# Where the layer norm of a convolution mixer is computed: beside the value projection or beside the key projection

## The chip, the cores and the metric

The kernel runs on one core of a Trainium2 chip. The metric is the device time of one execution in microseconds (us), the median of several runs. Engine names are those of the profile: PE is TensorE (its weight loads are listed apart as PEld), DVE is VectorE, ACT is ScalarE, POOL is GpSimd, SP is SyncE, which issues the DMAs.

## The reference, cut to what matters

One decoder layer for a sequence of 1024 tokens and a width of 1024, in float32. A joint input projection feeds four mixers of width 256 each; their outputs are concatenated, projected, added to the input, and a gated feed-forward block follows. The change concerns the third mixer (convolution, then layer norm and silu) and where it stands beside the fourth (attention):

```python
h = rms_norm(x, norm1_g)
z = h @ w_in
z_pool, s_b, s_c, s_h, c_a, c_g, zq, zk, zv = jnp.split(z, idx, axis=-1)
...
u = c_a * jax.nn.sigmoid(c_g)
u = causal_dwconv(u, conf_dw_w) + conf_dw_b
y_conf = jax.nn.silu(layer_norm(u, conf_ln_g, conf_ln_b))
...
y_attn = diff_attention(q, k, v, q_norm_g, k_norm_g, lam, lam_init, subln_g, rel_bias)
mix = jnp.concatenate([y_pool, y_sconv, y_conf, y_attn], axis=-1)
x = x + mix @ w_out
```

## The kernel before, in words

Every matmul is written as three (lines 138 to 140): each float32 operand is split into a high part and a low remainder, and high times high, high times low and low times high are added up in PSUM.

**Stages.** The tokens are eight blocks of 128, handled as four pairs p = 0 to 3. First come the norm and the channel-major projections of the three smaller mixers, with the long convolution (31 taps) on DVE; its result lies in `mixC`, channels on partitions. Then follow three token-major projections by `proj_tok` (line 468): keys (`use_k`), queries (`use_q`), values (`use_v`). For each pair `proj_tok` issues 48 matmuls of 128x256 and then calls its `use`. For keys and queries, `qk_norm` (line 482) copies the result out of PSUM, squares it (ACT), sums the squares (DVE, line 488), takes the power -1/2 on POOL (line 144, tile `r`) and scales (DVE, line 490); `stack_T` (line 493) splits the result and transposes it on PE (line 505). After the values, attention runs as 16 units `unit(u, p, h)` (line 652), one for each pair p and head h: scores on PE (line 668), bias and extremum on DVE (lines 675, 676), the exponential on ACT (line 679), the combination of the two maps on DVE (line 683), transposes on PE (line 694), their split on ACT and DVE (lines 698, 699), and the product with the values (line 703); after every second head the result is transposed back (line 715).

**What is moved.** `ln_pair(p)` takes the 256 tokens of pair p of `mixC` through layer norm and silu. It goes through five steps on four engines, each waiting for the one ahead:

```python
T.transpose(pt_[...], mixC[:, c, t * P:(t + 1) * P], ident)   # PE, L539, 4 of them
V.bn_stats(b6, pt_[...]); V.bn_aggr(mv[:, i, :], b6)          # DVE, L542, L543
rsqrt(rs, mv[:, :, 1], 1.0, 2)                                # POOL, L143, L144
V.tensor_scalar(ln[:, i, :], pt_[...], mv[...], rs[...])      # DVE, L548
T.transpose(pt_[...], ln[:, i, c * P:(c + 1) * P], ident)     # PE, L552, 4 of them
A.activation(th[:, c, :], src, AF.Tanh, ...)                  # ACT, L557
V.tensor_scalar(z, src, ...); V.scalar_tensor_tensor(z, ...)  # DVE, L558, L559
```

Its PSUM tile `lnp` has a single buffer, and its tile `th` shares the four buffers of tag `sp` with the keys' `kst` tiles and with the `sp` tiles named next.

**Filler work.** The part of the output projection that needs no attention is a generator, `gen_partial` (line 603). For each block of 128 tokens it splits the three finished mixer results `mixA`, `mixB` and `mixC` into `sp` tiles (ACT, DVE or POOL, lines 120, 122 and 622), issues 18 matmuls of 128x512 into PSUM tile `fm` (lines 599 to 601), and adds the input to the sum (lines 627, 628). `fill1` (line 636) hands these matmuls out between the instructions of the attention units, so many at each place as the table `FQ` says, and none of them may be issued ahead of the instruction at its place. Their weights are split in `wsplit` (tiles `whi` and `wlo`, line 134 on POOL).

**What sets the order.** All engines work through their instructions in order. The order is set at build time by a list scheduler: priority is the order in which the code issues, and an instruction that is not yet ready by the scheduler's own timing is passed over for a later one. So a filler matmul that has to wait for `mixC` slides to a later place on PE.

Of the kernel before, what the change touches and what calls it, by code (L numbers as in the profile page):

```python
# [66 lines left out]
def tile_hybrid(ctx, tc, x, norm1_g, w_in, pool_w, pool_scale, sconv_w, conf_w, conf_b, ln_g, ln_b,  # L67
# [74 lines left out]
    def rsqrt(dst, src, scale, n):  # L142
        G.tensor_scalar(dst, src, scale, EPS, op0=ALU.mult, op1=ALU.add)  # L143
        G.tensor_tensor(dst, dst, mhalf[:, 0:n], op=ALU.pow)  # L144
# [337 lines left out]
    def qk_norm(ps, z):  # L482
        A.copy(z, ps)
        sq = sm.tile([P, 512], F, name="sq", tag="sq")
        A.activation(sq, z, AF.Square)
        r = sm.tile([P, 16], F, name="r16", tag="r16", bufs=2)
        zv = z.rearrange("p (m d) -> p m d", d=32)
        V.tensor_reduce(r, sq.rearrange("p (m d) -> p m d", d=32), axis=AX.X, op=ALU.add)
        rsqrt(r, r, 1.0 / 32, 16)
        V.tensor_tensor(zv, zv, r.unsqueeze(2).broadcast_to([P, 16, 32]), op=ALU.mult)  # L490
        return zv

    def stack_T(kn, dst, isq, ps_new, nm, g, fill=None, p=None):
        for i in range(2):
            st = misc.tile([P, 4, 128], R, name="kst", tag="mi") if isq else spp.tile([P, 4, 128], R, name="kst", tag="sp")
            sv = st.rearrange("p m (a b d) -> p m a b d", a=2, b=2)
            src = kn[:, i, g * P:(g + 1) * P].rearrange("p (m d) -> p m d", d=32).unsqueeze(2).broadcast_to([P, 4, 2, 32])
            hi = sv[:, :, 0, :, :] if isq else sv[:, :, :, 0, :]
            lo = sv[:, :, 1, :, :] if isq else sv[:, :, :, 1, :]
            A.copy(hi, src)  # L500
            (G if isq and X3[2 * PO.index(p) + g] else V).tensor_tensor(lo, src, hi.bitcast(F), op=ALU.subtract)
            for m in range(0, 4, nm):
                ps = ps_new()
                for a in range(nm):
                    ins = T.transpose(ps[:, a * P:(a + 1) * P], st[:, m + a, :].bitcast(F), ident)
                if fill:
                    fill(ins)
                A.copy(dst[:, m:m + nm, i * P:(i + 1) * P], ps[:, 0:nm * P].rearrange("p (a b) -> p a b", a=nm))
# [5 lines left out]
        stack_T(qn[p], QT[p, g], True, ps_new, nm, g, fill, p)  # L514

    def use_k(p, ps):
        kn = qn[p]
        qk_norm(ps, kn.rearrange("p a b -> p (a b)"))
        for g in range(2):
            stack_T(kn, KT[g][:, :, p * 256:(p + 1) * 256], False, ps_t2, 4, g)  # L520
# [3 lines left out]
        V.tensor_tensor(qv, qv, gq.unsqueeze(1).broadcast_to([P, 16, 32]), op=ALU.mult)  # L524

    def use_v(p, ps):
        ln_pair(p)
        src = ps.rearrange("p (a d) -> p a d", d=64)
        vv = VV[p].rearrange("p i h d -> p (i h) d")
        A.copy(vv[:, :, 0:64], src)  # L530
        V.tensor_tensor(vv[:, :, 64:128], src, vv[:, :, 0:64].bitcast(F), op=ALU.subtract)

    def ln_pair(p):
        pt_ = psl.tile([P, 512], F, name="lnp", tag="lnp")
        mv = sm.tile([P, 2, 2], F, name="mv", tag="mv", bufs=2)
        for i in range(2):
            t = 2 * p + i
            for c in range(2):
                T.transpose(pt_[:, i * 256 + c * P:i * 256 + (c + 1) * P], mixC[:, c, t * P:(t + 1) * P], ident)  # L539
        for i in range(2):  # L540
            b6 = sm.tile([P, 6], F, name="b6", tag="b6", bufs=2)
            V.bn_stats(b6, pt_[:, i * 256:(i + 1) * 256])  # L542
            V.bn_aggr(mv[:, i, :], b6)  # L543
        rs = sm.tile([P, 2], F, name="rs", tag="rs", bufs=2)
        rsqrt(rs, mv[:, :, 1], 1.0, 2)
        ln = sm.tile([P, 2, 256], F, name="ln", tag="kn")
        for i in range(2):
            V.tensor_scalar(ln[:, i, :], pt_[:, i * 256:(i + 1) * 256], mv[:, i, 0:1], rs[:, i:i + 1],  # L548
                            op0=ALU.subtract, op1=ALU.mult)
        for c in range(2):  # L550
            for i in range(2):
                T.transpose(pt_[:, c * 256 + i * P:c * 256 + (i + 1) * P], ln[:, i, c * P:(c + 1) * P], ident)  # L552
        th = spp.tile([P, 2, 256], F, name="th", tag="sp")
        for c in range(2):
            z = mixC[:, c, p * 256:(p + 1) * 256]
            src = pt_[:, c * 256:(c + 1) * 256]
            A.activation(th[:, c, :], src, AF.Tanh, bias=lb[:, c:c + 1], scale=lg[:, c:c + 1])  # L557
            V.tensor_scalar(z, src, lg[:, c:c + 1], lb[:, c:c + 1], op0=ALU.mult, op1=ALU.add)  # L558
            V.scalar_tensor_tensor(z, th[:, c, :], 1.0, z, op0=ALU.add, op1=ALU.mult)  # L559

    proj_tok(C_K, use_k)
    proj_tok(C_Q, use_q, PO)
    for g in range(2):
        prep_q(PO[0], g, ps_t2, 4)
    proj_tok(C_V, use_v)

    hstk.close()
# [253 lines left out]
    for u in range(16):  # L821
        j, h = u // 4, u % 4
        p = PO[j]
# [355 lines left out]
```

## Time and profile before

| | us |
|---|---|
| median of 3 runs (lowest to highest) | 1107.63 (1106.45 to 1109.91) |
| the profiled execution | 1103.38 |
| its span, first to last instruction | 1101.6 |
| PE busy | 1059.2 |
| DVE busy | 739.1 |
| ACT busy | 440.5 |
| POOL busy | 223.2 |

The profiled execution is 4.25 us below the median of the runs. Busy times are sums over instructions; matmuls overlap one another in the pipeline, so PE busy is not PE at its peak. The stages that matter here are the token-major projections, which run from 172.5 to 251.7 us of the span, and the attention units behind them. The line that ends the sixth unit is the third group of line 715 matmuls.

### The profile page before, as it was taken

The page shows a single profiled execution, that of the slowest core. Times are in us where ns is not written, and L with a number is a line of the kernel's source. Part 1 is how long each engine was busy: PE and PEld are TensorE (multiplying, and loading weights), DVE is VectorE, ACT ScalarE, POOL GpSimd, SP SyncE. Part 2 cuts the span into 40 slices and gives each one's busy share as a digit, 9 for nine tenths or more (in the row PEclk, how much of TensorE's full clock was granted, in tenths as well). Part 3 has the DMA queues.
Part 4 walks back from the last instruction along what each step waited for, and adds up shares of the span by engine and source line. Part 5 has one row for each costly group of instructions (what it writes and reads, how often), then busy time and mean ns, then how long its engine had stood idle before and what let it go on. Part 6 is the DMA issues. An engine that isn't in the chain of part 4 may idle for free.

```text
span 1101.6 us, 13525 instructions
## 1 busy us (share of the span) xinstructions
PE 1059.2 (96%) x5203; PEld 882.0 (80%) x5203; DVE 739.1 (67%) x1127; ACT 440.5 (40%) x710; POOL 223.2 (20%) x202
## 2 busy tenths in 40 slices
PE   7989999997998989999999999999999999999998
PEld 7858889995777877777878888888888888888887
DVE  5599973458779996598667676565555656655540
ACT  5511213634567676542323333332333343433320
POOL 5224323653667653201000000000000000000000
PEclk9989999996999999999999999999999999999999
DMA  8131120110012121013567773233133168866731
GB/s 224 36 96 39 39 58 20 40 40 20 29 41 75 39 67 58 20 39 116 186 239 259 252 258 104 78 124 125 58 125 124 67 211 288 278 197 196 236 113 39
DMA packets 89664, 128.04 MB, mean 116 GB/s; under 512 B 17112, under 2 KB 57600, under 8 KB 87040
## 3 DMA queue, kind: packets, MB, share of 16 engines
q1 hardware_dynamic: 89600, 127.18, 35.4%
q8 instruction: 41, 0.67, 0.2%
q14 instruction: 23, 0.19, 0.1%
HBM read 94.13 MB, written 33.04 MB: 115 GB/s over the span
## 4 chain that ended last, share of the span: by engine, by line
PE 80%; DVE 9%; DMA 6%; ACT 2%; SPq 1%; POOL 1%; issue 1%; ACTq 0%; POOLq 0%; DVEq 0%
PE sb L140 10%; PE sb L138 10%; PE sb L139 10%; PE mm L140 6%; PE mm L139 6%; PE mm L138 6%; PE dx L138 3%; PE dx L139 3%; PE dx L140 3%; PE dy L139 2%; PE dy L138 2%; PE dy L140 2%; DMA dT<-wd 2%; PE fm L599 2%; DMA wd<-in_w_down_dram 2%; PE fm L601 2%
## 5 line engine op out<-in xcount | busy, mean ns | idle before, releaser
L138 PE MATMUL sb<-T,rhi 128*128 128x512 f32 x320 | 125.5, 392 | 0.0
L139 PE MATMUL sb<-T,rhi 128*128 128x512 f32 x320 | 125.4, 392 | 0.0
L140 PE MATMUL sb<-T,rlo 128*128 128x512 f32 x320 | 125.4, 392 | 0.0
L906 DVE TENSOR_TENSOR dq<-ds,dq 128x2048 fp32r<-128x2048 f32 x35 | 80.0, 2290 | 60.6 <-ACT dq L905 60.6
L905 ACT CAST dq<-ds 128x2048 fp32r<-128x2048 f32 x35 | 66.8, 1911 | 105.5 <-PE dy L140 39.5
L134 POOL TENSOR_TENSOR wlo<-st,whi 128x1024 fp32r<-128x1024 f32 (+2 forms) x30 | 73.9, 2466 | 103.9 <-ACT whi L120 97.6
L139 PE MATMUL mm<-hT,whi 128*128 128x512 f32 (+1 forms) x224 | 82.3, 372 | 0.7 <-DVE hT L200 0.7
L140 PE MATMUL mm<-hT,wlo 128*128 128x512 f32 (+1 forms) x224 | 81.9, 369 | 0.0
L138 PE MATMUL mm<-hT,whi 128*128 128x512 f32 (+1 forms) x224 | 80.0, 373 | 1.0 <-ACT hT L199 1.0
L312 DVE SCALAR_TENSOR_TENSOR t<-u,cw,t 128x1023 f32<-128x1023 f32 (+28 forms) x58 | 71.2, 1268 | 0.7
L139 PEld LDWEIGHTS sb<-T,rhi 128*128 128x128 f32 x320 | 60.1, 188 | 13.5
L138 PEld LDWEIGHTS sb<-T,rhi 128*128 128x128 f32 x320 | 60.1, 188 | 13.5 <-DVE tp L1025 0.3
L140 PEld LDWEIGHTS sb<-T,rlo 128*128 128x128 f32 x320 | 60.0, 188 | 13.5
L905 ACT CAST rhi<-st 128x1024 fp32r<-128x1024 f32 x28 | 29.4, 1051 | 85.6 <-PE sb L139 44.6
L140 PE MATMUL dx<-dq 128*128 128x512 f32 x160 | 62.3, 390 | 0.0
L139 PE MATMUL dx<-dq 128*128 128x512 f32 x160 | 62.2, 389 | 0.0
L138 PE MATMUL dx<-dq 128*128 128x512 f32 x160 | 61.8, 389 | 0.0
L138 PE MATMUL mm<-whi,hT 128*128 128x256 f32 x192 | 55.0, 288 | 0.0
L140 PE MATMUL mm<-whi,hT 128*128 128x256 f32 x192 | 54.9, 287 | 0.0
L679 ACT ACTIVATE pt<-sc,mx 128x128 f32<-128x128 f32 (+7 forms) x64 | 47.6, 745 | 17.6 <-DVE mx L676 17.1
L139 PE MATMUL mm<-wlo,hT 128*128 128x256 f32 x192 | 54.5, 284 | 0.0
L120 ACT CAST whi<-st 128x1024 fp32r<-128x1024 f32 x28 | 29.4, 1049 | 61.6 <-PE mm L139 50.2
(342 smaller groups left out, 2705.2 us busy)
## 6 DMA issues: line engine op xcount, KB each, us to landing
ds<-dL SPq DMA_DIRECT2D x35, 512.0 KB, 4.1
wd<-in_w_down_dram SPq DMA_DIRECT2D x10, 1024.0 KB, 5.0
dT<-wd SPq DMA_DIRECT2D x10, 1024.0 KB, 4.0
dL<-afs SPq DMA_DIRECT2D x10, 1024.0 KB, 3.9
ds<-dT SPq DMA_DIRECT2D x20, 512.0 KB, 5.7
st<-in_w_in_dram SPq DMA_DIRECT2D x18, 512.0 KB, 3.8
st<-in_w_gate_dram SPq DMA_DIRECT2D x15, 512.0 KB, 4.1
st<-in_w_up_dram SPq DMA_DIRECT2D x15, 512.0 KB, 3.6
```

Source lines behind the costliest of these rows:

```text
L120: A.copy(dst, src)
L134: G.tensor_tensor(lo[:, nv:], st[:, nv:], hi[:, nv:].bitcast(F), op=ALU.subtract)
L138: T.matmul(ps, lhsT=L[0], rhs=Rr[0], start=first, stop=False, skip_group_check=more)
L139: T.matmul(ps, lhsT=L[0], rhs=Rr[1], start=False, stop=False, skip_group_check=more)
L140: return T.matmul(ps, lhsT=L[1], rhs=Rr[0], start=False, stop=last, skip_group_check=more)
L312: V.scalar_tensor_tensor((z if s == 30 else acc)[:, s:], u[:, :S - s], w[:, 30 - s:31 - s], acc[:, s:], op0=ALU.mult, op1=ALU.add)
L599: yield lambda: T.matmul(ps, lhsT=L[0], rhs=Rr[0], start=first, stop=False)
L601: yield lambda: T.matmul(ps, lhsT=L[1], rhs=Rr[0], start=False, stop=last)
L679: A.activation(pts[m][:, 0:w], sc[:, 0:w], AF.Exp, bias=mx, scale=-1.0, accum_out=lt[:, h, m, i:i + 1])
L905: A.copy(hi, src)
L906: (eng or V).tensor_tensor(lo, src, hi.bitcast(F), op=ALU.subtract)
```

## The change

The call of `ln_pair(p)` moves from the head of `use_v` to the head of `use_k`: the layer norm of a pair is now issued with the keys of that pair and ahead of what the keys need, rather than with its values. No instruction is added, dropped or changed in size.

```diff
     def use_k(p, ps):
+        ln_pair(p)
         kn = qn[p]
         qk_norm(ps, kn.rearrange("p a b -> p (a b)"))
...
     def use_v(p, ps):
-        ln_pair(p)
         src = ps.rearrange("p (a d) -> p a d", d=64)
```

The scheduler turns this into another order on PE, DVE, ACT and POOL; the DMA queue of SP stays the same. First, PE where the value projection (`mm`) ends and attention (`sc`) begins, before: `lnp` is the layer norm's PSUM tile, and no filler matmul (`fm`) is near.

```order
L140 MATMUL mm<-whi,hT_104 128x256
L668 MATMUL sc<-KT_1364,QT 128x256 x2
L539 MATMUL lnp<-ident,mixC 128x128 x4
L668 MATMUL sc<-KT_1364,QT 128x256 x3
L694 MATMUL tp<-ident,pt 128x128
L668 MATMUL sc<-KT_1364,QT 128x256 x2
L694 MATMUL tp<-ident,pt 128x128 x2
L552 MATMUL lnp<-ident,ln 128x128 x4
L703 MATMUL av<-at,VV_1375 128x256
```

The same place on PE in the changed kernel:

```order
L140 MATMUL mm<-whi,hT_104 128x256
L668 MATMUL sc<-KT_1364,QT 128x256
L599 MATMUL fm<-whi,sp 128x512
L600 MATMUL fm<-wlo,sp 128x512
L601 MATMUL fm<-whi,sp 128x512
L599 MATMUL fm<-whi,sp 128x512
L600 MATMUL fm<-wlo,sp 128x512
L601 MATMUL fm<-whi,sp 128x512
L599 MATMUL fm<-whi,sp 128x512
L668 MATMUL sc<-KT_1364,QT 128x256 x2
```

The transposes of pairs 2 and 3 (16 matmuls into `lnp`) have left the attention stage, and filler matmuls stand between the first scores. Up to the first group of line 715 there were 0 filler matmuls and are now 36; up to the second 54 and now 58; up to the third 101 in both. From there on the two orders of PE are alike but for a few neighbours that change places.

Second, POOL in the projections, before: `r_...` are the keys' sums of squares, one tile for each pair, `rs` is the layer norm's own, `wlo` a low part of weights.

```order
L143 TENSOR_SCALAR rs<-mv 128x2
L144 TENSOR_TENSOR rs<-rs,mhalf 128x2
L143 TENSOR_SCALAR r_1447<-r_1447 128x16
L144 TENSOR_TENSOR r_1447<-r_1447,mhalf 128x16
L143 TENSOR_SCALAR r_1540<-r_1540 128x16
L144 TENSOR_TENSOR r_1540<-r_1540,mhalf 128x16
L143 TENSOR_SCALAR r_1633<-r_1633 128x16
L144 TENSOR_TENSOR r_1633<-r_1633,mhalf 128x16
L134 TENSOR_TENSOR wlo<-st,whi 128x1024 x2
```

And POOL there in the changed kernel:

```order
L143 TENSOR_SCALAR r_1598<-r_1598 128x16
L143 TENSOR_SCALAR rs<-mv 128x2
L144 TENSOR_TENSOR r_1598<-r_1598,mhalf 128x16
L144 TENSOR_TENSOR rs<-rs,mhalf 128x2
L143 TENSOR_SCALAR r_1720<-r_1720 128x16
L144 TENSOR_TENSOR r_1720<-r_1720,mhalf 128x16
L134 TENSOR_TENSOR wlo<-st,whi 128x1024 x2
L143 TENSOR_SCALAR rs<-mv 128x2
L143 TENSOR_SCALAR r_1842<-r_1842 128x16
L144 TENSOR_TENSOR rs<-rs,mhalf 128x2
L144 TENSOR_TENSOR r_1842<-r_1842,mhalf 128x16
```

The layer norm's small steps on POOL now stand behind the keys' powers and, for pair 2, behind two weight splits. On PE the projections now hold all 32 transposes of `lnp` instead of 16. Between the last line 539 matmul of a pair and its first line 552 matmul PE now has 66 projection matmuls and 16 transposes of line 505 for pair 1, 49 and 8 for pair 2, 42 and 8 for pair 3, and 48 projection matmuls for pair 0.

## Rows read from the trace of the kernel before

**Rows 1.** From the page: busy times; granted clock in 40 slices.
```profile
PE 1059.2 (96%) x5203; PEld 882.0 (80%) x5203; DVE 739.1 (67%) x1127; ACT 440.5 (40%) x710; POOL 223.2 (20%) x202
...
PEclk9989999996999999999999999999999999999999
```

**Rows 2.** Stretches: length, busy us and instructions of PE, PEld, DVE, ACT, POOL; clock.
```profile
172.50:251.70 79.20, 79.20 (x670) 78.93 (x669) 38.31 (x63) 35.62 (x70) 40.47 (x29) 1.00 0.11 34
...
251.70:311.40 59.70, 49.41 (x232) 40.28 (x231) 47.11 (x156) 33.15 (x96) 34.90 (x43) 0.83 0.10 29
```

**Rows 3.** PE in time at three places: start, duration, line, tiles, count.
```profile
251.71 0.41 PE L668 MATMUL sc<-KT,QT 128*128 128x256 f32 x2
...
278.63 0.63 PE L599 MATMUL fm<-whi,sp 128*128 128x512 f32 x1
...
311.25 0.60 PE L715 MATMUL tp<-ident,oT 128*128 128x128 f32 x4
```

**Rows 4.** Waits of PE from 251.7 to 311.4: total us, times, longest.
```profile
PE sc L668 <- ACT pt L679: 5.8, 4, 2.4
```

**Rows 5.** Stretches in which the clock was halved, columns as in rows 2.
```profile
256.65:273.70 17.05, 12.86 (x49) 10.10 (x50) 13.49 (x57) 9.10 (x31) 3.05 (x7) 0.50 0.05 17
277.10:280.50 3.40, 3.23 (x9) 2.65 (x10) 2.54 (x11) 1.53 (x5) 0.73 (x1) 0.50 0.00 0
```

**Rows 6.** The chain: one group of `lnp` transposes at full clock.
```profile
240.58 0.44 PE lnp L539 x4
```

**Rows 7.** DVE groups of the layer norm, 251.7 to 311.4: busy us, mean ns.
```profile
L558 DVE TENSOR_SCALAR mixC<-lnp,lg,lb 128x256 f32<-128x256 f32 x4 | 2.1, 538 | 0.0
L559 DVE SCALAR_TENSOR_TENSOR mixC<-th,mixC 128x256 f32<-128x256 f32 x4 | 2.0, 502 | 0.0
L548 DVE TENSOR_SCALAR ln<-lnp,mv,rs 128x256 f32<-128x256 f32 x4 | 2.0, 537 | 0.0
...
L542 DVE BATCH_NORM_STATS2 b<-lnp 128x6 f32<-128x256 f32 x4 | 1.5, 418 | 0.5 <-PE lnp L539 0.5
...
L543 DVE BATCH_NORM_AGGREGATE mv<-b 128x2 f32<-128x6 f32 x4 | 0.5, 160 | 0.0
```

**Rows 8.** Layer norm of pair 1 in time, from its first PE to its DVE step.
```profile
240.42 0.60 PE L539 MATMUL lnp<-ident,mixC 128*128 128x128 f32 x4
...
243.66 1.00 DVE L548 TENSOR_SCALAR ln<-lnp,mv,rs 128x256 f32<-128x256 f32 x2 [1.10 <-POOL rs L144]
```

**Rows 9.** POOL groups, 172.5 to 251.7: busy us, mean ns.
```profile
L144 POOL TENSOR_TENSOR r<-r,mhalf 128x16 f32<-128x16 f32 x8 | 23.3, 2914 | 0.7
L134 POOL TENSOR_TENSOR wlo<-st,whi 128x1024 fp32r<-128x1024 f32 x6 | 14.9, 2485 | 14.8 <-ACT whi L120 9.3 <-DVE whi L122 5.4
```

**Rows 10.** POOL and DVE in time where both split operands.
```profile
197.50 5.04 POOL L134 TENSOR_TENSOR wlo<-st,whi 128x1024 fp32r<-128x1024 f32 x2 [0.47 <-ACT whi L120]
...
198.84 3.99 DVE L501 TENSOR_TENSOR kst<-qn,kst 128x256 fp32r<-128x256 f32 x2 [1.09 <-ACT kst L500]
...
203.34 0.75 DVE L501 TENSOR_TENSOR kst<-qn,kst 128x256 fp32r<-128x256 f32 x2
```

**Rows 11.** Two stretches of attention behind the sixth unit, columns as in rows 2.
```profile
311.40:350.00 38.60, 32.71 (x190) 26.67 (x188) 33.75 (x90) 28.27 (x65) 25.82 (x22) 1.00 0.18 60
350.00:400.00 50.00, 50.00 (x288) 43.22 (x287) 46.52 (x103) 35.15 (x72) 29.91 (x34) 1.00 0.15 49
```

**Rows 12.** Two filler matmuls in time at full clock.
```profile
281.77 0.39 PE L599 MATMUL fm<-whi,sp 128*128 128x512 f32 x1
282.00 0.40 PE L600 MATMUL fm<-wlo,sp 128*128 128x512 f32 x1
```

**Rows 13.** Six units in three stretches that end at line 715; columns as rows 2.
```profile
251.70:269.50 17.80, 10.53 (x42) 7.64 (x40) 15.82 (x60) 8.42 (x29) 6.03 (x6) 0.64 0.10 30
269.50:294.10 24.60, 21.85 (x95) 18.00 (x96) 17.96 (x62) 13.51 (x40) 13.30 (x18) 0.85 0.07 22
294.10:311.40 17.30, 17.03 (x98) 14.65 (x97) 13.32 (x35) 11.21 (x28) 15.56 (x20) 1.00 0.13 36
```

## The prediction

> **What bounds the kernel now.** I read the page first. PE is busy 96% of the span, DVE 67%, and the row of granted clocks has its dips at the start and in the tenth slice, where the attention stage begins [rows 1]. So PE's order is what counts, and the place to look at is where PE has gaps or a low clock. Then I read the stretches. In the token-major projections, 172.5 to 251.7 us, PE is busy all of the 79.2 us, at 0.118 us for each of its 670 instructions, while DVE is busy 38.3 and POOL 40.5 us [rows 2]. In the first six attention units, 251.7 to 311.4 us, PE is busy 49.4 of 59.7 us, so 10.3 us are gaps, and the mean clock is 0.83 [rows 2]. The timeline shows why: the first scores run at 251.7 us, the first filler matmul at 278.6 us [rows 3]. In these 27 us PE has little but the units' own chain to do (score, extremum on DVE, exponential on ACT, back to PE), and its longest sum of waits is 5.8 us for the exponential [rows 4]. The filler matmuls need `mixC`, whose layer norm for pairs 2 and 3 is still being worked on between the units.
>
> The clock tells the same. PE runs with 1.00, the upper of its two levels (2.4 GHz), in the projections; in the first 5 us of attention it is mostly idle; then the clock is at 0.50 (1.2 GHz) from 256.65 to 273.70 us and again from 277.10 to 280.50 us [rows 5]. Behind 280.5 us, with filler matmuls on PE, it stays at 1.00. The two stretches at 0.50 hold 12.86 + 3.23 = 16.1 us of busy PE.
>
> **The change, part by part.** The profiled execution took 1103.38 us, 1.8 us of it outside its span; the sum is made against it, and I carry its difference over to the median of the runs, 1107.63 us, 4.25 us higher.
>
> *Work that goes to the projections.* The 16 transposes of pairs 2 and 3 now run there. PE is full there, so they lengthen the stage: four groups of four at 0.44 us [rows 6] are 1.8 us, plus 1.8 us on the end. DVE gets 2.1 + 2.0 + 2.0 + 1.5 + 0.5 = 8.1 us more [rows 7], and ACT four `th` steps; with 38.3 us of 79.2 used, DVE has room, so I cost this at nothing, as the projection matmuls cover it, unless PE has to wait for it, which is the next term.
>
> *A wait that may be added.* PE takes its instructions in order, so behind a line 552 transpose that waits for `ln` stand the projection matmuls of the next pairs, and all the later stages behind them. In the trace the way from the first line 539 matmul to the end of line 548 takes 240.42 to 244.66, 4.2 us [rows 8]. PE now has 82 instructions between them for pair 1, 57 for pair 2, 50 for pair 3 and 48 for pair 0: at 0.118 us, 9.7, 6.7, 5.9 and 5.7 us of cover. POOL's `rs` steps, however, now stand behind the keys' power of 2.9 us [rows 9]. If that is in the way each time, the chain is 7.1 us: 0.4 us short for pair 2 and 1.2 us for pair 3. Lower bound 0, upper bound of this case 1.6; neither row is nearer, so I take 0.8 us.
>
> On DVE there is a row that speaks against the move: two line 501 steps took 3.99 us while POOL split weights for 5.04 us, and 0.75 us right after [rows 10], 3.2 us more. The Trainium skill, "SBUF — State Buffer", section "Who interferes with whom", gives a reason: a DVE instruction with two SBUF inputs and a GpSimd instruction that reads SBUF use one shared port pair, and the one that starts first holds it throughout. By that rule line 559, with `th` and `mixC` as inputs, can be held up too, and there is more of POOL's long work beside it in the projections; the trace agrees for line 501. By the row, and by the rule, the sum stays as it is as long as the layer norm is not what PE waits for; if it is, this is the last rival below.
>
> *Work that leaves the first six units, and the fillers.* The fillers' inputs are ready when attention begins: 36 of the 101 filler matmuls stand in the first two units instead of none, and 101 in all six as before. What PE has to do there: 49.4 us, less half of the 16.1 us at half clock (8.0), less the 1.8 us of moved transposes, leaves 39.6 us. DVE: 47.1 less 8.1 leaves 39.0 us. How long do they take together? Lower bound: PE without a gap, 39.6 us. Two stretches right behind show units and fillers interleaved from a table at full clock [rows 11]: from 350 to 400 us PE has no gap and DVE is 93% busy, which would give 39.0 / 0.93 = 41.9 us; from 311.4 to 350 us PE is 85% busy and DVE 87%, which would give 39.6 / 0.847 = 46.7 us. Upper bound: the gaps stay, 59.7 less 1.8 = 57.9 us. The nearest row is the stretch that follows at once, with units as small as these: I take 46.7 us. That is 13.0 us less than 59.7.
>
> The weights for the fillers are split at the start of attention (DVE `whi`, then POOL `wlo`) as before; the first filler group has its weights from the queries' buffers and doesn't wait for them. The second and third groups wait for a POOL split of 2.5 us each [rows 9]; I cost that inside the 85%.
>
> *Sum.* 13.0 − 1.8 − 0.8 = 10.4 us less: 1093.0 for an execution like the profiled one, 1097.2 for the median. Behind the sixth unit PE's order is the same, so what is won there is not given back: the feed-forward part is bound by PE without gaps, whenever it starts.
>
> **The rivals.**
>
> *The fillers get in the way.* A filler that stands ahead of a score or a transpose on PE delays the unit's chain, and at 0.23 us apiece [rows 12] 36 of them are 8.3 us in a stretch that took 17.8 us [rows 13]. If none of it falls into gaps, the first two units take 26.1 us; the second stretch, with 22 instead of 54 fillers, is 7.4 us shorter and the third 0.9 us, and nothing is won by filling. What is left is the clock: 8.0 − 1.8 − 0.8 = 5.4 us, 1102.2 us. For it: the chain's steps are short and each needs PE four times. Against it: POOL, ACT and DVE all have gaps in 251.7 to 269.5 us, and PE 7.3 us of them [rows 13].
>
> *The clock falls all the same.* The first scores still wait for DVE behind the two `whi` casts, and later fillers for POOL; if PE has a gap like that of 251.7 to 256.65 us again, the 8.0 us are not won: 13.0 − 8.0 − 2.6 = 2.4 us, 1105.2 us. Against it: seven fillers stand between the first and the second score.
>
> *Better than the sum.* PE and DVE as from 350 to 400 us: 59.7 − 41.9 − 1.8 = 16.0 us less, 1091.6; without any gap 18.3, 1089.3.
>
> *Slower: the layer norm stalls the projections.* Place: the line 552 transposes of pairs 1 to 3. Price: if `rs` waits for a power (2.9) and for two weight splits (5.0), and DVE is held up once (3.2), the chain is 4.2 + 11.1 = 15.3 us, and PE waits 5.6 + 8.6 + 9.4 = 23.6 us. That leaves 13.0 − 1.8 − 23.6 = −12.4: 1120 us. It decides from the point where the three waits together exceed 11.2 us, that is, a chain of about 11 us for each pair on average. For it: POOL's order has `rs` of pair 2 behind two splits. Against it: that is one pair of four, and POOL is busy only half of the stage.
>
> **How the numbers follow.** Forecast and better 0.64, fillers in the way 0.17, clock falls 0.10, both of these 0.03 (the 2.6 us of cost alone, 1110.2), slower 0.06. A measurement of this kernel can tell 0.3%, 3.3 us, from no change: faster means below 1104.3, slower above 1111.0. The first two cases are faster, less a small part of the second: 0.78. The clock's case and both together are no change: with that part 0.15. Slower: 0.07. The forecast's own range is 1091 to 1102; to leave out no more than 2 in 10 the range reaches from 1090, near the gapless bound, to 1105.5, past the clock's case.
>
> **What would show it.** In the changed profile: line 552 matmuls of all pairs before the end of the values, which should come some 2 to 3 us later than 251.7; first filler right behind the first score; clock at 1.00 from the start of attention; third group of line 715 at about 301 us instead of 311.25; the rest shifted as a block. Wrong: waits of line 552 on `ln` of several us in the projections, a stretch at 0.50 behind 254 us, or waits of the scores and transposes that grow by as much as the fillers take.

## The result and the profile after

| | before | after |
|---|---|---|
| median (lowest to highest), us, 4 runs each | 1107.04 (1104.86 to 1109.91) | 1091.78 (1088.75 to 1097.45) |
| profiled execution, us | 1103.38 | 1092.04 |
| first line 539 matmul of the projections to first score | 80.91 | 82.56 |
| first score to third group of line 715 (six units) | 59.54 | 45.35 |
| third group of line 715 to the end of the span | 790.35 | 789.9 |

The changed kernel takes 0.9867 of the time of before, 95% interval 0.9820 to 0.9913: 15.3 us between the medians. The forecast was 1097.2 us, the range 1090 to 1105.5.

In the page after, PE and the granted clock answer to [rows 1]. DVE and PE are busy some 5 us less in all, and the dip of the clock in the tenth slice is gone.

```profile
span 1090.2 us, 13509 instructions
...
PE 1054.3 (97%) x5203; PEld 875.9 (80%) x5203; DVE 734.6 (67%) x1127; ACT 439.4 (40%) x710; POOL 224.1 (21%) x202
...
PEclk9989999999999999999999999999999999999999
```

The stretches of the changed kernel, with the columns of [rows 2] (length, then busy us and instructions of PE, PEld, DVE, ACT, POOL, then clock, DMA share, GB/s): the projections, the six units, the three parts of the units that end at line 715 (they answer to [rows 13]), and the one piece at half clock (it answers to [rows 5]).

```profile
172.40:255.00 82.60, 82.60 (x694) 81.62 (x693) 44.49 (x84) 38.75 (x77) 47.70 (x38) 1.00 0.11 33
255.00:300.30 45.30, 41.94 (x214) 33.07 (x213) 38.78 (x129) 28.84 (x87) 30.45 (x34) 0.96 0.13 41
...
255.00:272.70 17.70, 14.96 (x66) 11.10 (x65) 14.16 (x50) 8.82 (x33) 9.77 (x9) 0.90 0.15 46
272.70:283.30 10.60, 10.24 (x58) 8.08 (x57) 9.21 (x33) 8.35 (x26) 6.16 (x7) 1.00 0.07 25
283.30:300.30 17.00, 16.75 (x94) 13.89 (x93) 15.41 (x47) 11.67 (x30) 14.52 (x19) 1.00 0.15 47
...
262.60:266.00 3.40, 3.40 (x13) 2.81 (x14) 2.09 (x10) 2.04 (x7) 0.08 (x1) 0.51 0.03 7
```

PE is still busy through the whole of the projections. The first and the third part of the units are about as long as before (17.7 and 17.0 us, against 17.8 and 17.3); nearly all of the gain is in the second, 10.6 us for 24.6. The first part takes no longer although 36 filler matmuls now run in it, and the second has work left for 10.6 us only. The gaps of PE in the units are 45.3 − 41.9 = 3.4 us instead of 10.3, and the clock is halved for 3.4 us instead of 20.5.

PE in time in the changed kernel (start, duration, line, tiles), which answers to [rows 3]: the filler runs right behind the first score, and line 715 comes at 300.33.

```profile
254.98 0.28 PE L668 MATMUL sc<-KT,QT 128*128 128x256 f32 x1
255.09 0.40 PE L599 MATMUL fm<-whi,sp 128*128 128x512 f32 x1
...
300.33 0.60 PE L715 MATMUL tp<-ident,oT 128*128 128x128 f32 x4
```

The waits of PE from 255 to 300.3 us in the changed kernel (what it waited for: us in all, times, longest) answer to [rows 4]. The wait for the exponential has shrunk from 5.8 to 1.5 us, and no other has taken its place.

```profile
PE tp L694 <- DVE pt L683: 1.5, 3, 0.8
PE sc L668 <- ACT pt L679: 1.5, 2, 0.8
PE tp L505 <- POOL kst L501: 0.3, 1, 0.3
```

**What the first filler waited for in the kernel before.** The prediction said: for `mixC`. The first filler matmul, however, belongs to token block 0, which is in pair 0, and the layer norm of pair 0 had ended in the projections (the last of its line 559 steps at about 234 us). In the kernel before, DVE and POOL in time show what came right before 278.63 us:

```profile
272.87 0.43 DVE L122 CAST sp<-mixC 128x256 fp32r<-128x256 f32 x1
...
275.25 0.72 POOL L622 TENSOR_TENSOR sp<-mixB,sp 128x256 fp32r<-128x256 f32 x1
...
277.65 0.54 DVE L558 TENSOR_SCALAR mixC<-lnp,lg,lb 128x256 f32<-128x256 f32 x1
```

DVE reads `mixC` for the filler's token block at 272.87 us, ahead of pair 3's last steps, and all operands of that block were split by 275.97 us (the first filler's own, the high part of `mixA`, by 273.56). At 278.19 us line 558 of pair 3 ends, the last instruction that reads `lnp`, and 0.44 us later the filler runs. PE shows no idle time right before it: the scheduler had put it behind the score that runs at 278.03 us, so this trace alone doesn't show what held it. PSUM space is given out by pools, in the order in which they are opened. The projections' pools end and attention's begin in the same space (lines 96 and 97, 575 to 577):

```python
psm = psA.enter_context(pool("psm", 3, space=PSUM))   # mm, three buffers
psl = psA.enter_context(pool("psl", 1, space=PSUM))   # lnp
...
psp = psB.enter_context(pool("psp", 2, space=PSUM))   # tp
psq = psB.enter_context(pool("psq", 1, space=PSUM))   # av
psf = psB.enter_context(pool("psf", 1, space=PSUM))   # fm: the fourth buffer, as lnp was
```

So `fm` would take over the buffer of `lnp` and have to wait until the layer norm of all pairs is through with it. That became the theory to test.

### The profile page after: what moved, and what is told of

Same layout as the page of the kernel before. It is cut to its first block, busy times and chain, and to the rows that moved or that the text cites. A ratio compares the mean times of both kernels' runs of the same rounds, so it can differ in the third digit from the quotient of the medians.

```text
span 1090.2 us, 13509 instructions
## 1 busy us (share of the span) xinstructions
PE 1054.3 (97%) x5203; PEld 875.9 (80%) x5203; DVE 734.6 (67%) x1127; ACT 439.4 (40%) x710; POOL 224.1 (21%) x202
## 4 chain that ended last, share of the span: by engine, by line
PE 78%; DVE 11%; DMA 6%; ACT 2%; issue 1%; POOL 1%; SPq 0%; ACTq 0%; POOLq 0%; DVEq 0%
PE sb L140 10%; PE sb L138 10%; PE sb L139 10%; PE mm L139 6%; PE mm L140 6%; PE mm L138 6%; PE dx L140 3%; PE dx L139 3%; PE dx L138 3%; PE dy L140 3%; PE dy L139 2%; PE dy L138 2%; DMA wd<-in_w_down_dram 2%; DMA dT<-wd 2%; DVE pt L683 1%
```

## The experiments

Three theories. B: the fillers wait for the PSUM buffer of `lnp`. M, that of the prediction: they wait for the data in `mixC`. L: the fillers' place matters little; the gain is that the layer norm's 8.1 us of DVE work [rows 7] leave the units. The first four kernels ran on one chip beside the kernel before (1107.25 us, 26 runs); the last four on another (1105.4 us, 13 runs).

**1. Layer norm of pairs 2 and 3 still in attention, in another buffer** (kernel before; the `tp` tiles, of which there are two).

```diff
     def use_v(p, ps):
-        ln_pair(p)
+        p < 2 and ln_pair(p)
...
-    def ln_pair(p):
-        pt_ = psl.tile([P, 512], F, name="lnp", tag="lnp")
+    def ln_pair(p, ps_n=None):
+        pt_ = ps_n() if ps_n else psl.tile([P, 512], F, name="lnp", tag="lnp")
...
+    ln_pair(2, ps_tp), ln_pair(3, ps_tp)
```

> The kernel before (layer norm beside the values), but pairs 2 and 3 are issued at the head of attention and take a buffer of the transposes' PSUM tile tp instead of lnp, so that the last reader of lnp is pair 1's and not pair 3's. The layer norm of pairs 2 and 3 stays among the attention units. Theory B (bank): the filler matmuls waited for lnp, because their tile fm takes over its PSUM bank; here fillers start right behind the first scores, the clock stays up, and most of the gain comes: 1095 to 1101 us against 1107, a little less than the change gives since 8.1 us of DVE work stay in the units. Theory M (the prediction's: fillers wait for mixC of pairs 2 and 3): fillers start as late as before, about 1105 to 1108. Theory L (load: what counts is that the layer norm's steps leave the units): 1105 to 1108.

Measured: 1098.88 us (1096.18 to 1100.36), ratio 0.9919 [0.9893, 0.9946]. The first filler comes 14.1 us behind the first score instead of 26.9, the units take 53.2 us, and the clock is halved for 13.7 us. The wait has not gone but moved, onto the buffer that the layer norm now uses. In its trace, PE in time (in brackets the idle time before, and what ended it):

```profile
266.28 0.88 PE L694 MATMUL tp<-ident,pt 128*128 128x128 f32 x3 [1.13 <-DVE mixC L558]
266.81 0.78 PE L599 MATMUL fm<-whi,sp 128*128 128x512 f32 x1
```

A unit's transposes wait for line 558, and the filler stands behind them. The filler runs ahead of the end of the last line 558, at 268.50 us, which fits B. But with two buffers the layer norm also ends earlier, 15.8 us behind the first score instead of 26.5, so this kernel doesn't tell the buffer from an earlier layer norm. The time lies in B's range, though B's fillers right behind the first scores did not show.

**2. Fillers that read no `mixC`** (kernel before).

```diff
-            for kg, mix in enumerate((mixA, mixB, mixC)):
+            for kg, mix in enumerate((mixA, mixB, mixB)):
```

> The kernel before, but the fillers read mixB a second time in place of mixC (so the output lacks the convolution mixer's part). Everything else, the layer norm beside the values too, stays. Theory M (fillers wait for mixC): fillers start at once at the beginning of attention and the time falls to 1093 to 1098 us. Theory B (bank of lnp): the first filler still stands behind the last layer norm step, near 278 us, and the time is 1104 to 1108 us. Theory L (load of the layer norm in the units): 1104 to 1108 us.

Measured: 1108.8 us (1103.29 to 1113.93), ratio 1.001 [0.9986, 1.0033]. In its trace, in time, the last split of an operand, line 558 of pair 3, and the first filler:

```profile
275.47 0.72 POOL L622 TENSOR_TENSOR sp<-mixB,sp 128x256 fp32r<-128x256 f32 x1
...
277.87 0.53 DVE L558 TENSOR_SCALAR mixC<-lnp,lg,lb 128x256 f32<-128x256 f32 x1
...
278.85 0.63 PE L599 MATMUL fm<-whi,sp 128*128 128x512 f32 x1
```

The fillers no longer need anything of the layer norm's result and still come behind its last reading of `lnp`, 26.9 us behind the first score as before. M is refuted as the cause. The time is 0.8 us above the range of B and L, which expected the same here, so this kernel doesn't tell the two apart.

**3. The changed kernel, fillers held back** (the first 26 entries of `FQ` are zero, the 27th is 52; the layer norm stays early).

```diff
-FQ = [13, 0, 1, 0, 4, 0, 0, 0, 0, 0, 5, 6, 1, 4, 0, 0, 0, 0, 6, 1, 2, 5, 1, 0, 3, 0, 0, 2, ...
+FQ = [0, 0, 0, 0, 0, 0, 0, 0, 0, 0, 0, 0, 0, 0, 0, 0, 0, 0, 0, 0, 0, 0, 0, 0, 0, 0, 52, 2, ...
```

> The changed kernel (layer norm beside the keys), but the table that hands out the fillers gives none at its first 26 places and all of these at the 27th, so that by the order PE has 0 fillers in the first two units, 58 up to the second and 101 up to the third group of line 715, nearly as before (0, 54, 101). Theory B and M (the gain is fillers in the gaps, with the clock that this holds up): most of the gain goes, 1102 to 1108 us, and the clock is at half again for 10 us or more behind 256 us. Theory L (load): it stays, 1090 to 1096 us.

Measured: 1097.32 us (1094.29 to 1102.35), ratio 0.9921 [0.9895, 0.9948], between the two. Its stretches, columns as above, in the three parts that end at line 715:

```profile
255.06:270.30 15.24, 8.56 (x29) 5.74 (x27) 12.15 (x46) 7.02 (x27) 4.84 (x3) 0.67 0.11 35
270.30:289.70 19.40, 19.38 (x93) 16.47 (x94) 10.63 (x38) 10.38 (x31) 10.87 (x13) 0.91 0.08 28
289.70:306.50 16.80, 16.68 (x94) 13.90 (x93) 15.40 (x47) 11.56 (x30) 15.12 (x19) 1.00 0.16 48
```

The first part has no filler, as before, and takes 15.2 us instead of 17.8 [rows 13]: 2.6 us are what the early layer norm gives there by itself. The second is 5.2 us shorter than before, partly since its fillers start 2.0 us behind its beginning instead of 9.2. The units are 8.1 us shorter in all, so L has a share. The rest of the 14.2 us is the fillers' place: 36 of them in the first part cost it 17.7 − 15.2 = 2.5 us and save 19.4 − 10.6 = 8.8 us in the second.

**4. The buffers exchanged** (kernel before; `psf` opened ahead of `psq`, so that `av` and not `fm` takes over the buffer of `lnp`).

```diff
-    psq = psB.enter_context(pool("psq", 1, space=PSUM))
     psf = psB.enter_context(pool("psf", 1, space=PSUM))
+    psq = psB.enter_context(pool("psq", 1, space=PSUM))
```

> The kernel before, but the PSUM pools of fm (fillers) and av (attention times values) are opened in the other order, so that av and not fm takes over the bank of lnp. Theory B (bank): the wait moves with the bank: the first av matmuls (line 703) stand behind the last layer norm step of pair 3, by the order after the last line 552, and the fillers ahead of them; the units' own chain is held instead, so the time is about as before or worse, 1102 to 1112 us. Theories M and L: nothing depends on the bank, av and fm start as before and the time is 1105 to 1108 us with line 703 first at about 261 us.

Measured: 1110.8 us (1109.27 to 1113.31), ratio 1.0032 [1.0013, 1.0052]. In its trace, in time:

```profile
268.99 0.40 POOL L122 CAST sp<-mixA 128x256 fp32r<-128x256 f32 x1
...
272.99 0.63 PE L599 MATMUL fm<-whi,sp 128*128 128x512 f32 x1
...
273.80 0.54 DVE L558 TENSOR_SCALAR mixC<-lnp,lg,lb 128x256 f32<-128x256 f32 x1
...
274.49 1.94 PE L703 MATMUL av<-at,VV 128*128 128x256 f32 x8 [0.45 <-DVE mixC L558]
```

Two lines of pool order have moved the wait from the fillers to the units' own product: `av`, which reads nothing of the layer norm, now stands idle until line 558 of pair 3 ends and comes at 274.49 us instead of 261.20, and the first fillers run ahead of it. This confirms that whichever tile takes the buffer over waits for the last reading of `lnp`. It also shows that the buffer was only a part of the delay: with it free, the first filler still comes 20.3 us behind the first score instead of 26.9. What it reads, the high part of `mixA`, is cast by POOL only at 268.99 us, right behind the late layer norm's `rs` steps (at 268.05 and 268.33 us), and on PE it stands behind a score at 272.61 us.

The second token block has a wait of its own. Its first `sp` tile is written 0.09 us behind the end of line 559 of pair 3, the last to read `th`, which shares the four buffers of tag `sp`: 274.89 and 274.80 us here, 279.27 and 279.18 in the kernel before, 263.02 and 262.93 in experiment 6. So the PSUM buffer was the last of the first filler's waits, and not the only one: the late layer norm held the fillers on POOL and in the `sp` buffers too.

**5. The changed kernel again**, as the measure for the three that follow.

> The changed kernel itself, as the reference for the other three on the same chip: 1090 to 1094 us, 12 to 17 us below the kernel before.

Measured: 1089.72 us (1088.58 to 1091.47), 0.3 us below the expected range, ratio 0.9866 [0.9837, 0.9894]; projections 82.44 us, units 44.96 us, half clock 3.4 us, the same again.

**6. Layer norm beside the queries** (`ln_pair(p)` at the head of `use_q`).

> The layer norm issued with the queries of a pair instead of the keys (head of use_q). By the order 36, 58 and 101 fillers stand ahead of the three groups of line 715, as in the changed kernel, but the last line 552 transposes stand behind the first two scores. Theory B (the fillers wait for the bank of lnp, whose last reader is the layer norm of pair 3): the bank comes free some 4 us into attention, so the gain is that of the changed kernel less 1 to 5 us: 1092 to 1098 us. Theory L (all that counts is that the layer norm's steps have left the units): as the changed kernel or 1 us above, 1091 to 1094 us. If the place beside the keys itself mattered (M): far from the changed kernel, above 1100 us.

Measured: 1100.42 us (1099.41 to 1104.48), ratio 0.9956 [0.9938, 0.9974]: less gain than B and L expected, and by the number alone in the range of the third case there, that the place beside the keys itself matters. In its trace, in time, with idle time and its end in brackets:

```profile
261.50 1.03 PE L668 MATMUL sc<-KT,QT 128*128 128x256 f32 x2 [2.97 <-ACT pt L679]
...
261.88 0.53 DVE L558 TENSOR_SCALAR mixC<-lnp,lg,lb 128x256 f32<-128x256 f32 x1
...
262.56 0.77 PE L599 MATMUL fm<-whi,sp 128*128 128x512 f32 x1
```

The layer norm of the last pair alone reaches into attention: its last transposes run at 255.18 us, its line 558 ends at 262.41, and the first filler follows 0.15 us later, 7.6 us behind the first score. PE waits 2.36 and 2.97 us for exponentials meanwhile, since DVE comes to their scores only behind casts of 2.31 us (`whi`) and 1.99 us (`sp`) that began inside splits of POOL's; the clock is halved for 10.2 us, and the units take 53.75 us. So two thirds of the gain, 10.7 us of 15.7, hang on the last pair's layer norm being over when attention begins. How much of that is the buffer and how much these casts isn't told apart.

**7. Layer norm at the end of the keys' work** (`ln_pair(p)` at the end of `use_k`).

> The layer norm issued with the keys, but behind what the keys need (at the end of use_k), so that the keys' chain has priority over it. Theories B and L: no difference to the changed kernel, 1090 to 1094 us, since PE didn't wait for either chain in the projections. If the layer norm ahead of the keys held the projections up: 1 to 3 us less than the changed kernel.

Measured: 1090.23 us (1088.41 to 1091.2), ratio 0.9867 [0.984, 0.9894]; projections 82.39 us, units 44.81 us. Nothing moved by as much as a measurement can tell: where in the keys' step it stands doesn't matter.

**8. The changed kernel, the high parts of the output projection's weights all cast by ACT** (to free DVE for the first scores).

```diff
-WOE = [0, 0, 1, 0, 1, 0, 0, 0]
+WOE = [0, 0, 0, 0, 0, 0, 0, 0]
```

> The changed kernel with the high parts of the fillers' second and third weight tile cast on ACT, which is idle there, instead of on DVE (table WOE all zero). In the changed kernel DVE casts them at 253.18 and 255.06 us, and its first step for the scores comes only at 256.89 us, behind the cast of 1.91 us. If these casts hold the start of attention, the first step of line 676 comes 1 to 2 us earlier and the time falls by as much, 1089 to 1092 us; if not, the same as the changed kernel within 1 us.

Measured: 1090.38 us (1088.69 to 1092.29), ratio 0.9876 [0.9842, 0.991], no difference from the changed kernel. DVE in time in its trace shows where the gain went:

```profile
252.76 0.30 DVE L676 CUSTOM_DVE_ANT_0 sc<-sc,tb 128x128 f32<-128x128 f32 x1 [4.69 <-PE sc L668]
...
255.71 1.64 DVE L122 CAST sp<-mixC 128x256 fp32r<-128x256 f32 x1 [0.85 <-PE fm L601]
257.27 0.29 DVE L676 CUSTOM_DVE_ANT_0 sc<-sc,tb 128x128 f32<-128x128 f32 x1
```

The first step of line 676 comes 0.3 us behind the first score (252.45) instead of 1.9, but the next only at 257.27 us, behind a cast that the fillers need and that takes 1.64 us beside a split of POOL's; the units take 46.3 us. The 1.6 us were given back at once. No kernel here is faster than the changed one.

## Why the prediction was right, and where not

**The failed step** is the sentence "The filler matmuls need `mixC`, whose layer norm for pairs 2 and 3 is still being worked on between the units." The layer norm was what held them, but not by its result: experiment 2 took the result away and nothing moved. The last wait of the first filler was for the PSUM buffer, and experiment 4 moved the buffer and the wait went with it; the 20.3 us that stayed there came before that, from the late `rs` steps on POOL ahead of the fillers' casts and from the order on PE, as far as the trace of experiment 4 shows; no run takes these away by themselves. That the forecast survived is luck: the change ends all these waits at once. With the wrong reason one would have expected a gain from fillers that need no `mixC`; experiment 2 shows that there is none.

**Projections**, forecast +1.8 and +0.8 for a stall: +1.65 us (+1.53 in the repeat), and the stall is zero. In the trace, PE waits for nothing from 172.4 to 255 us. The tightest case is pair 2, whose `rs` stands behind two weight splits. In time in the changed kernel:

```profile
200.35 5.45 POOL L134 TENSOR_TENSOR wlo<-st,whi 128x1024 fp32r<-128x1024 f32 x2 [1.43 <-ACT whi L120]
...
200.61 0.42 DVE L559 SCALAR_TENSOR_TENSOR mixC<-th,mixC 128x256 f32<-128x256 f32 x1
...
207.17 0.99 DVE L548 TENSOR_SCALAR ln<-lnp,mv,rs 128x256 f32<-128x256 f32 x2 [2.16 <-POOL rs L144]
...
209.73 0.60 PE L552 MATMUL lnp<-ident,ln 128*128 128x128 f32 x4
```

DVE waited 2.16 us for `rs`, as the slower rival feared, but `ln` is ready at 208.16 and needed at 209.73 us, with 1.6 us to spare (2.4 to 2.6 us for the other pairs). So the splits and the keys' powers ahead of `rs` cost PE nothing here. The layer norm's line 559 was not held up on DVE beside POOL either, the other fear behind that rival. It took a mean of 424 ns in the projections before and 419 ns after, with eight instead of four of them, and line 501 went from 600 down to 453 ns. By the rule of the Trainium skill, "SBUF — State Buffer", section "Who interferes with whom", a step with two inputs in SBUF is stopped when POOL's split got to the ports first. The line 559 step shown above starts 0.26 us behind POOL and takes no longer than the others, so by this row the rule did not hold it. The pair of splits takes 5.45 us, and the next such pair, at 231.07, 4.80: here it may have been POOL that waited, which isn't shown.

**Six units**, forecast −13.0: −14.2 us (−14.6 in the repeat), mis-sized by 1.2. The forecast took 85% of PE from the stretch that follows at once; the units reached 41.94 of 45.3 us, 93%, between that and the gapless stretch [rows 11]. Of the 14.2 us, 6.9 are gaps and the rest less busy time of PE: the 1.8 us of moved transposes, and half clock given back. How much is the freed DVE and how much the fillers' place can be told only in part (experiment 3): about 8.1 us with the fillers held to 17.2 us behind the first score, some of it because that is still 9.7 us earlier than before, and 6.1 us for the fillers in place.

**Clock at 1.00 from the start of attention**: nearly. One piece of 3.4 us at 0.51 is left. It begins at 262.6 us, behind two gaps of PE in the 3 us before it (in time, PE, changed kernel):

```profile
260.79 0.33 PE L694 MATMUL tp<-ident,pt 128*128 128x128 f32 x1 [0.81 <-DVE pt L683]
...
262.05 0.86 PE L668 MATMUL sc<-KT,QT 128*128 128x256 f32 x2 [0.70 <-ACT pt L679]
```

In the kernel before, a mostly idle PE in the first 5 us (1.37 us busy of 4.95) was followed by 17 us at half clock [rows 5]. The rival in which the clock falls all the same did not come about. The seven fillers between the first scores, its argument against, fit what experiment 3 shows: without fillers in the first part the clock there was 0.67, with them 0.90.

**Fillers in the way**: refuted by the first part, 17.7 us where that rival had 26.1. Against the first part of experiment 3, which has no fillers, the 8.3 us of fillers at 0.23 us [rows 12] made it 2.5 us longer and filled 3.9 us of gaps (15.24 − 8.56 there, 17.70 − 14.96 here); the remaining 1.9 us are, as an estimate, what the higher clock gave back.

**Shape of the trace**: line 715 at 300.33 us, forecast about 301, and so near only because this execution's projections start 1.6 us later; end of the values 1.65 us later, measured from the projections' own start, forecast 2 to 3; the part behind the units 790.35 and 789.9 us, shifted as a block.

**The sum.** In the profiled executions: −14.2 + 1.65 − 0.45 for the rest, and +1.6 since the projections of this execution start 1.6 us later, ahead of anything that was changed: −11.4 us of span, forecast −10.4. The medians differ by 15.3 us, and in the repeat the spans by 14.8 (+0.9, +1.5, −14.6, and −2.6 in the rest). The units and projections give 12.5 to 13.0 us of that. The remaining 2 to 3 us of the medians lie in parts that the change doesn't touch. They are no more than the intervals leave open (9.6 to 19.9 us here, 11.7 to 18.0 in experiment 5), and their cause stays open; the profiled execution of before, 1103.38 us, lies below all four runs. That the measured 1091.78 us is beside the 1091.6 of the case better than the sum is luck too: that case had the units at 41.9 us, and they took 45.35.

## What to carry to other kernels

A buffer handed from one stage's pool to the next is a dependency that no line of the code shows: if the first instructions of a stage are late though their data is ready, look for what last read the space they write. Work that straggles over a stage border costs more than its own busy time when filler work stands behind it; move all of it ahead of the border, since the last pair alone kept two thirds of the cost (experiment 6). And look for what ended just ahead of a late instruction before writing why it is late, then test it: 278.19 beside 278.63 us was in the profile from the start, and exchanging two buffers (experiment 4) showed what it meant and how much of the delay it was.

## What the runs showed of the hardware

A cast on DVE from float32 into the form that PE reads stood still while POOL split weights. In the changed kernel, DVE and POOL in time:

```profile
253.18 0.69 DVE L122 CAST whi<-st 128x1024 fp32r<-128x1024 f32 x1 [2.57 <-PE mm L139]
254.01 2.41 POOL L134 TENSOR_TENSOR wlo<-st,whi 128x1024 fp32r<-128x1024 f32 x1 [10.96 <-PE mm L140]
255.06 1.91 DVE L122 CAST whi<-st 128x1024 fp32r<-128x1024 f32 x1 [1.19 <-PE mm L139]
```

The cast takes 0.69 us alone. Begun inside the split it ends at 256.97 us, 0.55 us behind the split's end, whenever it began: in the kernel before it took 2.38 us and in experiment 6 2.31, and each ended 0.55 us behind the split there. The cast `sp` takes 0.28 us alone, 1.64 us in experiment 8 and 1.99 in experiment 6, and both times it ended 0.15 to 0.16 us behind POOL's split. So it is stopped for as long as the split lasts and not slowed. The Trainium skill, "SBUF — State Buffer", section "Who interferes with whom", counts casts, under conditions on their operands, among the steps that can contend with GpSimd for the shared ports, and has the later of the two fully blocked; the trace agrees. The prediction weighed that rule for line 559 alone, where it changed nothing, and not for the casts that stand ahead of the first scores.
